# Hyena's inverse transforms in radix-2 steps with tokens in the rows, its bias as a product with ones, and its projection in three passes of 256 columns

## The chip, the cores and the metric

The kernel runs on one core of a Trainium2 chip. The metric is the device time of one execution in microseconds. All data are float32; matmuls take each operand as a pair of rounded parts (high and low).

## What is computed

Two layers of a hybrid backbone over 256 latent tokens of width 2048. Layer 0 (state space and attention) and both FFNs are not touched. Layer 1 is a bidirectional order-2 Hyena long convolution:

```python
proj = dwconv_centred(u @ w_in + b_in, short_w, short_b)      # 3 x 2048 channels, 3 taps
x1, x2, y = proj[..., :d], proj[..., d:2 * d], proj[..., 2 * d:]
for i, gate in enumerate((x1, x2)):
    h_two = einsum('lf,fkd->lkd', hid, fw_out[:, i]) * window
    k = concat(h_two[:, 0], 0, flip(h_two[1:, 1]));  k = k / sum(|k|)
    y = gate * (irfft(rfft(y, 512) * rfft(k, 512))[:256] + fbias[i] * y)
return y @ w_out + b_out
```

## The kernel before

A product of two split operands is three matmuls (`mm3`, lines 372 to 374): high x high, high x low, low x high, added up in one PSUM tile. Weights come from HBM as 1 MB tiles and are split on the chip: ScalarE copies the rounded high part (line 339), VectorE subtracts it (line 340). `run` walks over a list of such tiles; it loads and splits two tiles ahead, and after each tile it advances a list of background generators by some ticks. A generator issues a piece of other work at each `yield`. The build's scheduler orders the instructions of each engine by priority, so pieces of the two streams interleave on TensorE.

There are three forms of a projection tile. `gemm` makes the three passes over 256 (or 258) columns into one accumulator. `wide` (lines 561, 562, 564) takes the high and the low part of the activations side by side as 512 columns against the high weights, and the low weights against 256 columns: two matmuls for each of the 16 blocks of the contraction, and two halves to be added at the end. `total` does that: ScalarE copies one half with the bias (line 573), VectorE adds the other (line 574). `gemm2` (line 819) is layer 0's own.

Layer 1: `ev_hy` makes 48 projection tiles of 128 channels (3 kinds x 16), each followed by the short filter of three taps (lines 1227 to 1229). The first 5 tiles (`HFOLD`) use the unnormalised input with `gemm` and are folded afterwards; 43 use `wide` and `total`. Tiles come in 8 groups of 256 channels. For each group `hyena_steps` runs in the background, once for each of two orders:
- four transposes bring y (channels in rows) to even and odd tokens in rows (line 1263), which are split;
- forward transforms of the even and of the odd tokens (12 matmuls each way, `ps_u`), sum and difference of the two give the two halves of the spectrum (lines 1277, 1278);
- each half is multiplied by the filter's spectrum, read back from HBM, and split into `ph`, `pl`;
- the inverse transform (`ps_c`), with channels in rows: for each of two halves of the channels, 4 spectrum blocks x 3 passes of 256 columns;
- y times the bias on ScalarE (line 1300), the inverse times 1/norm added to it (line 1301), and the gate's product (line 1302), on VectorE.

In the startup a generator `filters` makes the filters of both orders for 4 x 512 channels, 8 rounds: products of 512 columns (`pss`), the window (line 755), splits, the sum of the absolute values (`am`), the spectra (`psk`, in `spectra`), which go to HBM, and 1/norm (`kinv`). It takes turns with generators for the modulation vectors (`ps_mod`), whose weights stream in, and the input norms. The stage after it starts when the filters' memory is free.

The modulation vectors for the later sub-layers are made on VectorE all along the kernel: one multiplication of 128x2048 (line 445) and 1 MB of weights for each 128 channels, 160 in all. `MODS` says how many are issued per 16 blocks of contraction in each of five stages (layer 0's two projections, FFN 0, hyena, FFN 1).

Of the kernel before, what the change touches and what calls it, by code (L numbers as in the profile page):

```python
# [37 lines left out]
MOD_HOLD = 3  # L38
MODS = (1.8, 0.6, 0.68, 0.08, 0.6)
TICKS = ((1, 1, 1), (1, 2), (4,))  # L40
# [131 lines left out]
def _prepare(inputs):  # L172
# [82 lines left out]
    a["hw_out"] = _tiles(g["hy_w_out"][0])  # L255
    fw = g["hy_fw_out"][0]
    a["fw"] = fw.transpose(1, 2, 0, 3).reshape(2, P, 4, 512).transpose(0, 2, 1, 3)
    hid = np.zeros((P, 3 * P), f32)
# [8 lines left out]
class _Kernel:  # L267
# [428 lines left out]
    def filters(self, pool):  # L696
# [31 lines left out]

        yield
        wt = None  # L730
        last = None
# [38 lines left out]
    def spectra(self, pool, fh, fl, gi, s2, am):  # L770

        nc = self.nc
        g, i = gi // 2, gi % 2
        for w in range(2):
            two = []
            for tt in (1, 0):
                ps = self.ps.tile([P, 512], F32, tag=("acc", "ms")[tt], name=self.nm("psk"), bufs=3)
                r = slice(w * P, (w + 1) * P)
                self.mm3(ps, (fh[:, tt, r], fl[:, tt, r]), (s2[w][0][:, tt], s2[w][1][:, tt]), True, True)
                two.append(ps)  # L780
            odd = pool.tile([P, 512], F32, tag="odd", name=self.nm("kodd"), bufs=1)
# [425 lines left out]
    def ev_hy(self, blocks, g, kind, i):  # L1207
# [17 lines left out]
        else:  # L1225
            t = self.total(self.wide(blocks, self.cols_of(self.need_n(self.hn))), self.col("hy_b_in", ci))
        nc.scalar.activation(o, t, AF.Identity, bias=self.col("short_b", ci), scale=self.col("short_w", 48 + ci))
# [22 lines left out]

    def hyena_steps(self, g):
        nc, hp = self.nc, self.hyp
        y = self.hyt[g, 0]
        for o in range(2):
            kf = hp.tile([P, 4, S], F32, tag="kf", name=self.nm("kf"), bufs=1)
            src = self.kscr[2 * (g // 2) + o].rearrange("p (a b) -> p a b", b=512)
            nc.sync.dma_start(kf, src[:, :, (g % 2) * S:(g % 2) * S + S])
            yth = hp.tile([P, 2, S], F32R, tag="yth", name=self.nm("yth"), bufs=1)
            ytl = hp.tile([P, 2, S], F32R, tag="ytl", name=self.nm("ytl"), bufs=1)
            pst = self.ps.tile([P, 2, S], F32, tag="ms", name=self.nm("ps_yT"))  # L1260
            for tt in range(2):
                for c in range(2):
                    nc.tensor.transpose(pst[:, tt, c * P:(c + 1) * P], y[:, c, tt::2], self.mat("ident"))
            self.split(yth, ytl, pst)
            yield from self.wait(1 + HWAITS[0])
# [12 lines left out]
            nc.vector.tensor_tensor(odd, psu[0], odd, ALU.subtract)  # L1278
            for f2, u in enumerate((ev, odd)):
                t = hp.tile([P, 2, S], F32, tag="t1", name=self.nm("t1"), bufs=2)  # L1280
# [3 lines left out]
                nc.vector.tensor_tensor(u[:, 1], u[:, 1], t[:, 0], ALU.add)  # L1284
                self.split(*[v.rearrange("p (r f) t -> p r f t", f=2)[:, :, f2] for v in (ph, pl)], u)
                yield
            yield from self.wait(HWAITS[1])
            while (g, 1 + o, 1) not in self.hy_done:
                yield
            if g == 0 and o == 1:  # L1290
                self.mh, self.ml, self.mhl = self.pair("hmix")
            for c in range(2):
                ch = 2 * g + c
                psc = self.ps.tile([P, 512], F32, tag="ms", name=self.nm("ps_c"))
                cs = slice(c * P, (c + 1) * P)
                for f4 in (0, 2, 1, 3):
                    self.mm3(psc[:, :S], (ph[:, f4, cs], pl[:, f4, cs]), (self.dih[:, f4], self.dil[:, f4]), f4 == 0, f4 == 3)
                yc = y[:, c, :]
                t = self.small.tile([P, S], F32, tag="ft", name=self.nm("yt"), bufs=3)
                nc.scalar.activation(t, yc, AF.Copy, scale=self.col("fbias", o * 16 + ch))  # L1300
                nc.vector.scalar_tensor_tensor(t, psc[:, :S], self.kinv[:, o * 16 + ch:o * 16 + ch + 1], t, ALU.mult, ALU.add)
                nc.vector.tensor_tensor(yc, t, self.hyt[g, 1 + o][:, c, :], ALU.mult)
                if o == 1:
                    self.split(self.mh[:, ch, :S], self.ml[:, ch, :S], yc)
            yield from self.wait(1 + HWAITS[2])
# [238 lines left out]
    def layer1(self):  # L1544
        nc, a, hp = self.nc, self.a, self.hyp
        self.hn = {}
        self.hyt = {}
# [65 lines left out]
```

## Time and profile before

| | |
|---|---|
| median of 3 runs | 2646.43 us (2644.79 to 2648.49) |
| profiled execution, time | 2648.55 us |
| its span | 2646.7 us |
| mean granted TensorE clock | 0.99 |
| startup | 0 to about 190 us |
| layer 0 and FFN 0 | about 190 to 1445 us |
| hyena with its projections | about 1445 to 1806 us |
| output projection and FFN 1 | about 1806 to 2647 us |

The span goes from the first to the last instruction. PE is TensorE's matmul stream, PEld its weight loads, DVE is VectorE, ACT ScalarE, POOL GpSimd and SP SyncE, which issues most DMAs.

### The profile page before, as it was taken

How to read it: one execution, taken by the hardware profiler on the slowest of the kernel's cores; microseconds unless marked ns; L12 is line 12 of the kernel's file. 1: busy time of each engine (PE TensorE's matmuls, PEld its weight loads, DVE VectorE, ACT ScalarE, POOL GpSimd, SP SyncE). 2: the span in 40 equal slices, each digit the busy share in tenths (PEclk: the TensorE clock that was granted, in tenths of full speed). 3: DMA queues.
4: the chain of work that ended last, by engine and by line, in shares of the span. 5: the costliest groups of instructions: out<-in, count | busy, mean ns of one | idle time of the engine just before them, and what ended most of it. 6: DMA issues, size and time to landing. Idle time of an engine off the chain costs nothing.

```text
span 2646.7 us, 39320 instructions
## 1 busy us (share of the span) xinstructions
PE 2572.2 (97%) x15128; PEld 2200.9 (83%) x15128; DVE 2088.8 (79%) x3178; ACT 1428.2 (54%) x2298; POOL 7.4 (0%) x22
## 2 busy tenths in 40 slices
PE   5979999999999999999999999999999999999997
PEld 2548779887988888888888888888998888888886
DVE  7867878777898888888889999898887656656656
ACT  4544656646654544544556755556654544544455
POOL 0000000000000000000000000000000000000000
PEclk9979999999999999999999999999999999999999
DMA  9956557556588887988887555456587654545543
GB/s 354 342 211 221 189 186 278 208 203 234 215 323 310 335 310 284 343 308 298 330 302 271 198 179 180 170 184 235 207 313 261 217 178 169 215 171 195 192 162 125
DMA packets 105610, 635.58 MB, mean 240 GB/s; under 512 B 11344, under 2 KB 19920, under 8 KB 44624
## 3 DMA queue, kind: packets, MB, share of 16 engines
q1 hardware_dynamic: 101904, 620.49, 64.3%
q10 hardware_dynamic: 2304, 8.39, 0.8%
q0 software_dynamic: 1216, 4.20, 0.5%
q8 instruction: 119, 1.95, 0.3%
q14 instruction: 67, 0.55, 0.1%
HBM read 622.55 MB, written 10.49 MB: 239 GB/s over the span
## 4 chain that ended last, share of the span: by engine, by line
PE 92%; DVE 4%; ACT 1%; issue 1%; DMA 1%; SPq 0%; DVEq 0%; ACTq 0%
PE acc L561 41%; PE acc L562 23%; PE acc L819 7%; PE acc L564 3%; PE acc L372 3%; PE acc L373 3%; PE acc L374 3%; PE ps_mod L1383 1%; DVE wlo L340 1%; PE ps_c L372 1%; PE ps_c L374 1%; PE ps_c L373 1%; DVE mraw L445 1%; PE ps_y L1070 0%; PE ps_o L1201 0%
## 5 line engine op out<-in xcount | busy, mean ns | idle before, releaser
L561 PE MATMUL acc<-act,whi 128*128 128x512 f32 x3525 | 1255.6, 396 | 3.9 <-ACT whi L339 3.9
L340 DVE TENSOR_TENSOR wlo<-raw,whi 128x1024 fp32r<-128x1024 f32 (+1 forms) x842 | 938.7, 1119 | 239.1 <-ACT whi L339 232.8
L339 ACT ACTIVATE whi<-raw 128x1024 fp32r<-128x1024 f32 (+1 forms) x842 | 814.6, 972 | 469.7 <-PE acc L561 244.5
L562 PE MATMUL acc<-act,wlo 128*128 128x256 f32 x3760 | 1020.7, 281 | 1.4 <-DVE wlo L340 1.4
L561 PEld LDWEIGHTS acc<-act,whi 128*128 128x128 f32 x3525 | 666.2, 189 | 150.4 <-ACT whi L339 4.9
L562 PEld LDWEIGHTS acc<-act,wlo 128*128 128x128 f32 x3760 | 709.3, 189 | 23.1 <-DVE wlo L340 2.9
L561 PE MATMUL acc<-hh,whi 128*128 128x512 f32 x1280 | 456.4, 395 | 0.0
L445 DVE SCALAR_TENSOR_TENSOR mraw<-mraw,cb 128x2048 f32<-128x2048 f32 x160 | 365.8, 2287 | 30.7 <-DMA mraw<-in_mod 30.4
L562 PE MATMUL acc<-hh,wlo 128*128 128x256 f32 x1408 | 376.2, 282 | 0.0
L561 PEld LDWEIGHTS acc<-hh,whi 128*128 128x128 f32 x1280 | 240.9, 188 | 51.0
L562 PEld LDWEIGHTS acc<-hh,wlo 128*128 128x128 f32 x1408 | 264.7, 188 | 11.5
L571 ACT ACTIVATE sum<-acc 128x256 f32<-128x256 f32 x160 | 61.5, 385 | 271.8 <-PE acc L564 271.8
L372 PE MATMUL acc<-act,whi 128*128 128x258 f32 (+1 forms) x560 | 160.4, 287 | 1.0 <-ACT act L500 1.0
L574 DVE TENSOR_TENSOR sum<-sum,acc 128x256 f32<-128x256 f32 x203 | 85.1, 419 | 96.1 <-ACT sum L571 95.8
L374 PE MATMUL acc<-act,wlo 128*128 128x258 f32 (+1 forms) x560 | 158.4, 284 | 0.9 <-DVE wlo L340 0.9
L373 PE MATMUL acc<-act,whi 128*128 128x258 f32 (+1 forms) x560 | 158.8, 284 | 0.0
L819 PE MATMUL acc<-act,whi 128*128 128x512 f32 x480 | 156.8, 404 | 0.0
L583 ACT ACTIVATE res<-acc,mcol 128x256 f32<-128x256 f32 x144 | 68.2, 474 | 135.5 <-PE acc L564 135.3
L586 DVE SCALAR_TENSOR_TENSOR res<-acc,mcol,res 128x256 f32<-128x256 f32 x160 | 77.1, 483 | 69.2 <-ACT res L583 59.7
L372 PEld LDWEIGHTS acc<-act,whi 128*128 128x128 f32 x560 | 106.6, 191 | 4.0 <-issue 2.5
L374 PEld LDWEIGHTS acc<-act,wlo 128*128 128x128 f32 x560 | 106.4, 190 | 2.0 <-DVE wlo L340 1.1
L373 PEld LDWEIGHTS acc<-act,whi 128*128 128x128 f32 x560 | 106.6, 190 | 1.4 <-issue 0.8
(333 smaller groups left out, 2754.3 us busy)
## 6 DMA issues: line engine op xcount, KB each, us to landing
raw<-in_w SPq DMA_DIRECT2D x176, 1024.0 KB, 4.9
mraw<-in_mod SPq DMA_DIRECT2D x160, 1024.0 KB, 5.1
raw<-in_w SPq DMA_DIRECT2D x128, 704.0 KB, 4.2
raw<-in_hw_in SPq DMA_DIRECT2D x48, 1024.0 KB, 4.8
raw<-in_w_in SPq DMA_DIRECT2D x29, 1024.0 KB, 5.0
mraw<-in_modn SPq DMA_DIRECT2D x19, 1024.0 KB, 9.0
raw<-in_w_o SPq DMA_DIRECT2D x16, 1024.0 KB, 4.8
raw<-in_hw_out SPq DMA_DIRECT2D x16, 1024.0 KB, 4.8
```

The lines of the kernel that those rows point to most:

```text
L339: nc.scalar.activation(hi, src, AF.Copy)
L340: nc.vector.tensor_tensor(lo, src, hi.bitcast(F32), ALU.subtract)
L372: t.matmul(out, lh, rh, start=first, stop=False)
L373: t.matmul(out, lh, rl, start=False, stop=False)
L374: t.matmul(out, ll, rh, start=False, stop=last)
L445: self.nc.vector.scalar_tensor_tensor(raw, raw, 1.0, self.cb, ALU.mult, ALU.mult, accum_out=self.mcol[:, j:j + 1])
L561: t.matmul(*high, start=kt == 0, stop=False, skip_group_check=True)
L562: t.matmul(ps[:, :S], wl, x[:, 0], start=False, stop=False, skip_group_check=True)
L564: t.matmul(*high, start=False, stop=True, skip_group_check=True)
L574: nc.vector.tensor_tensor(v, v, halves[0], ALU.add)
L586: nc.vector.scalar_tensor_tensor(v, halves[0], gate, v, ALU.mult, ALU.add)
L819: t.matmul(ps.rearrange("p (a b) -> p a b", a=2), w, self.act[:, j, :, kt, :S], start=kt == 0 and k == 0, stop=kt == n - 1 and k == 2)
```

## The change

- The inverse transform is done with frequencies against tokens: the two halves of the spectrum are added and subtracted first (VectorE), so that even tokens need only the sum and odd tokens only the difference. The tables, read at every second token, are the stationary operand, the spectra the moving one; tokens come out in the rows.
- Order 0: the gate is transposed to the same layout, multiplied there, and the product is the input of order 1 as it stands. Order 1: the result is transposed back, multiplied by its gate and split.
- The bias term becomes part of the filter's spectrum: bias x sum of absolute values, as a product of a matrix of ones with a row on each partition, is added to the even part of each spectrum. 1/norm is multiplied into the short filter's taps and bias of the two gates.
- `ev_hy` uses `gemm` over 256 columns in place of `wide` and `total`.
- `MODS`: 0.68 to 0.72 in FFN 0, 0.08 to 0 in hyena.

```diff
-MODS = (1.8, 0.6, 0.68, 0.08, 0.6)
+MODS = (1.8, 0.6, 0.72, 0.0, 0.6)
...
+    fb = g["hy_fbias"][0].reshape(2, 4, 512).transpose(1, 0, 2).reshape(8, 1, 512)
+    a["fbrow"] = np.broadcast_to(fb, (8, P, 512))
...
+        self.ones_r = pool.tile([P, P], F32R, name="ones_r")
+        nc.scalar.activation(self.ones_r, self.mat("ones"), AF.Copy)
...
+        fb = pool.tile([P, 512], F32, tag="fwr", name=self.nm("fb"), bufs=2)
+        nc.gpsimd.dma_start(fb, self.a["fbrow"][gi])
+        nc.vector.tensor_tensor(fb, fb, am, ALU.mult)
+        fx = [pool.tile([P, 512], F32R, tag=t, name=self.nm("fx"), bufs=2) for t in ("fwh", "fwl")]
+        self.split(*fx, fb)
...
-                self.mm3(ps, (fh[:, tt, r], fl[:, tt, r]), (s2[w][0][:, tt], s2[w][1][:, tt]), True, True)
+                self.mm3(ps, (fh[:, tt, r], fl[:, tt, r]), (s2[w][0][:, tt], s2[w][1][:, tt]), True, w == 1 or tt == 1)
+                if w == 0 and tt == 0:
+                    for k in range(2):
+                        nc.tensor.matmul(ps, self.ones_r, fx[k], start=False, stop=k == 1)
...
-            t = self.total(self.wide(blocks, self.cols_of(self.need_n(self.hn))), self.col("hy_b_in", ci))
+            ps = self.gemm(blocks, *self.need_n(self.hn)[:2], S)
+            t = self.small.tile([P, S], F32, tag="ft", name=self.nm("sum"), bufs=3)
+            nc.scalar.activation(t, ps[:, :S], AF.Identity, bias=self.col("hy_b_in", ci))
...
+        def by_tokens(v):
             pst = self.ps.tile([P, 2, S], F32, tag="ms", name=self.nm("ps_yT"))
             for tt in range(2):
                 for c in range(2):
-                    nc.tensor.transpose(pst[:, tt, c * P:(c + 1) * P], y[:, c, tt::2], self.mat("ident"))
-            self.split(yth, ytl, pst)
+                    nc.tensor.transpose(pst[:, tt, c * P:(c + 1) * P], v[:, c, tt::2], self.mat("ident"))
+            return pst
+
+        src = by_tokens(self.hyt[g, 0])
+        for o in range(2):
...
+            self.split(yth, ytl, src)
...
-                self.split(*[v.rearrange("p (r f) t -> p r f t", f=2)[:, :, f2] for v in (ph, pl)], u)
                 yield
+            t = hp.tile([P, 2, S], F32, tag="t1", name=self.nm("dif"), bufs=2)
+            nc.vector.tensor_tensor(t, ev, odd, ALU.subtract)
+            nc.vector.tensor_tensor(ev, ev, odd, ALU.add)
+            self.split(*parts[0], ev)
+            self.split(*parts[1], t)
...
+            if o == 0:
+                gate = hp.tile([P, 2, S], F32, tag="t1", name=self.nm("gate"), bufs=2)
+                nc.scalar.activation(gate, by_tokens(self.hyt[g, 1]), AF.Copy)
+            psc = self.ps.tile([P, 2, S], F32, tag="ms", name=self.nm("ps_c"))
+            for tt in range(2):
+                for k, r in enumerate((0, 2)):
+                    w = [d[:, r, tt::2] for d in (self.dih, self.dil)]
+                    self.mm3(psc[:, tt], w, (ph[:, r + tt], pl[:, r + tt]), k == 0, k == 1)
+            if o == 0:
+                nc.vector.tensor_tensor(gate, psc, gate, ALU.mult)
+                src = gate
+                continue
+            yt = hp.tile([P, 2, S], F32, tag="t1", name=self.nm("yt"), bufs=2)
+            nc.scalar.activation(yt, psc, AF.Copy)
+            yield
...
-                for f4 in (0, 2, 1, 3):
-                    self.mm3(psc[:, :S], (ph[:, f4, cs], pl[:, f4, cs]), (self.dih[:, f4], self.dil[:, f4]), f4 == 0, f4 == 3)
-                yc = y[:, c, :]
-                t = self.small.tile([P, S], F32, tag="ft", name=self.nm("yt"), bufs=3)
-                nc.scalar.activation(t, yc, AF.Copy, scale=self.col("fbias", o * 16 + ch))
-                nc.vector.scalar_tensor_tensor(t, psc[:, :S], self.kinv[:, o * 16 + ch:o * 16 + ch + 1], t, ALU.mult, ALU.add)
-                nc.vector.tensor_tensor(yc, t, self.hyt[g, 1 + o][:, c, :], ALU.mult)
-                if o == 1:
-                    self.split(self.mh[:, ch, :S], self.ml[:, ch, :S], yc)
+                for tt in range(2):
+                    nc.tensor.transpose(pst[:, c, tt::2], yt[:, tt, c * P:(c + 1) * P], self.mat("ident"))
+            yc = self.hyt[g, 0]
+            nc.vector.tensor_tensor(yc, pst, self.hyt[g, 2], ALU.mult)
+            for c in range(2):
+                self.split(self.mh[:, 2 * g + c, :S], self.ml[:, 2 * g + c, :S], yc[:, c])
...
+        for v in [self.col("short_w", 48 * k, 32) for k in range(3)] + [self.col("short_b", 0, 32)]:
+            nc.vector.tensor_tensor(v, v, self.kinv, ALU.mult)
```

## Rows read from the trace of the kernel before

**Rows 1.** The page, parts 1 and 4.
```profile
PE 2572.2 (97%) x15128; PEld 2200.9 (83%) x15128; DVE 2088.8 (79%) x3178; ACT 1428.2 (54%) x2298; POOL 7.4 (0%) x22
...
PE 92%; DVE 4%; ACT 1%; issue 1%; DMA 1%; SPq 0%; DVEq 0%; ACTq 0%
```

**Rows 2.** By stage: us, busy time of each engine, granted clock, DMA share, GB/s.
```profile
20.00:60.00 40.00, 31.72 (x118) 13.91 (x119) 31.36 (x72) 23.33 (x51) 1.07 (x2) 0.91 0.91 357
60.00:110.00 50.00, 46.59 (x248) 25.91 (x247) 42.73 (x85) 25.51 (x44) 2.14 (x4) 1.00 0.97 369
110.00:160.00 50.00, 33.93 (x164) 17.98 (x162) 36.15 (x70) 25.02 (x40) 0.19 (x2) 0.84 0.67 247
...
190.00:1410.00 1220.00, 1214.25 (x7156) 1048.02 (x7155) 1011.31 (x1444) 654.64 (x1053) 0.52 (x4) 1.00 0.74 270
1410.00:1440.00 30.00, 29.12 (x170) 25.41 (x169) 27.63 (x46) 19.25 (x36) 0.00 (x0) 1.00 0.70 245
1440.00:1480.00 40.00, 38.00 (x283) 35.64 (x282) 38.57 (x73) 29.85 (x58) 0.00 (x0) 1.00 0.59 224
...
1500.00:1790.00 290.00, 289.93 (x1809) 257.38 (x1808) 267.61 (x460) 163.71 (x254) 0.00 (x0) 1.00 0.50 178
```

**Rows 3.** Timeline of PE, one tile of hyena's projection, first and last step.
```profile
1624.19 0.39 PE L561 MATMUL acc<-act,whi 128*128 128x512 f32 x1
...
1629.13 0.39 PE L561 MATMUL acc<-act,whi 128*128 128x512 f32 x1
```

**Rows 4.** Timeline of PE, layer 0's z projection, eighteen steps apart.
```profile
424.91 0.28 PE L372 MATMUL acc<-act,whi 128*128 128x256 f32 x1
...
431.35 0.28 PE L372 MATMUL acc<-act,whi 128*128 128x256 f32 x1
```

**Rows 5.** Timeline of PE, inverse transform, first and last of 24.
```profile
1613.53 0.28 PE L372 MATMUL ps_c<-dih,ph 128*128 128x256 f32 x1
...
1616.28 0.28 PE L374 MATMUL ps_c<-dih,pl 128*128 128x256 f32 x1
```

**Rows 6.** Timeline of PE, four transposes and what follows.
```profile
1630.30 0.65 PE L1263 MATMUL ps_yT<-mats,hyt 128*128 128x128 f32 x4
1630.70 0.36 PE L374 MATMUL ps_c<-dih,pl 128*128 128x256 f32 x1
1630.90 0.28 PE L372 MATMUL ps_c<-dih,ph 128*128 128x256 f32 x1
```

**Rows 7.** Groups by line and shape, 1500 to 1790 us: busy, mean ns, idle before.
```profile
L373 PEld LDWEIGHTS ps_c<-dil,ph 128*128 128x128 f32 x117 | 22.2, 190 | 0.4
...
L574 DVE TENSOR_TENSOR sum<-sum,acc 128x256 f32<-128x256 f32 x39 | 16.2, 416 | 0.0
...
L1301 DVE SCALAR_TENSOR_TENSOR yt<-ps_c,kinv,yt 128x256 f32<-128x256 f32 x30 | 14.2, 481 | 0.7 <-PE ps_c L374 0.4
...
L1277 DVE TENSOR_TENSOR even<-ps_u,odd 128x512 f32<-128x512 f32 x14 | 9.6, 687 | 5.6 <-ACT odd L1275 5.5
...
L445 DVE SCALAR_TENSOR_TENSOR mraw<-mraw,cb 128x2048 f32<-128x2048 f32 x4 | 9.1, 2287 | 0.0
...
L1275 ACT ACTIVATE odd<-ps_u 128x512 f32<-128x512 f32 x14 | 8.3, 592 | 8.3 <-PE ps_u L374 8.3
```

**Rows 8.** Groups by line and shape, 0 to 190 us.
```profile
L339 ACT ACTIVATE fwh<-fwr 128x512 fp32r<-128x512 f32 x8 | 5.0, 626 | 4.4 <-PE pss L374 4.0 <-DMA fwr<-in_fw 0.4
```

**Rows 9.** The chain in the startup: start us, us, what.
```profile
28.36 0.43 PE pss L372
...
67.24 0.23 PE psk L374
...
157.63 2.50 ACT act L1456 x6
```

**Rows 10.** VectorE's timeline in the startup.
```profile
67.49 1.89 DVE L340 TENSOR_TENSOR sl<-sv,sh 128x512 fp32r<-128x512 f32 x3
```

**Rows 11.** The chain at the start of hyena.
```profile
1461.92 2.21 DVE mraw L445 x2
```

**Rows 12.** Groups by line and shape, 1400 to 1850 us.
```profile
L455 DVE TENSOR_TENSOR mcol<-mcol,cols 128x16 f32<-128x16 f32 x1 | 0.2, 171 | 0.0
```

More of the change, by code (lines that the diff above doesn't have):

```diff
@@ L1252, in hyena_steps @@
         nc, hp = self.nc, self.hyp
[L1253 to L1259, printed above, removed]
+        def by_tokens(v):
             pst = self.ps.tile([P, 2, S], F32, tag="ms", name=self.nm("ps_yT"))
@@ L1262, in hyena_steps @@
                 for c in range(2):
-                    nc.tensor.transpose(pst[:, tt, c * P:(c + 1) * P], y[:, c, tt::2], self.mat("ident"))
-            self.split(yth, ytl, pst)
+                    nc.tensor.transpose(pst[:, tt, c * P:(c + 1) * P], v[:, c, tt::2], self.mat("ident"))
+            return pst
+        src = by_tokens(self.hyt[g, 0])
+        for o in range(2):
+            kf = hp.tile([P, 4, S], F32, tag="kf", name=self.nm("kf"), bufs=1)
+            scr = self.kscr[2 * (g // 2) + o].rearrange("p (a b) -> p a b", b=512)
+            nc.sync.dma_start(kf, scr[:, :, (g % 2) * S:(g % 2) * S + S])
+            yth = hp.tile([P, 2, S], F32R, tag="yth", name=self.nm("yth"), bufs=1)
+            ytl = hp.tile([P, 2, S], F32R, tag="ytl", name=self.nm("ytl"), bufs=1)
+            self.split(yth, ytl, src)
             yield from self.wait(1 + HWAITS[0])
@@ L1278, in hyena_steps @@
             nc.vector.tensor_tensor(odd, psu[0], odd, ALU.subtract)
-            for f2, u in enumerate((ev, odd)):
+            both = (ev, odd)
+            parts = [[v.rearrange("p (r f) t -> p r f t", f=2)[:, :, f2] for v in (ph, pl)] for f2 in range(2)]
+            for f2, u in enumerate(both):
                 t = hp.tile([P, 2, S], F32, tag="t1", name=self.nm("t1"), bufs=2)
@@ L1289, in hyena_steps @@
                 yield
-            if g == 0 and o == 1:
+            if o == 0:
[13 more added lines that the diff above has]
+            yield
+            if g == 0:
                 self.mh, self.ml, self.mhl = self.pair("hmix")
+            pst = self.ps.tile([P, 2, S], F32, tag="ms", name=self.nm("ps_yC"))
             for c in range(2):
-                ch = 2 * g + c
-                psc = self.ps.tile([P, 512], F32, tag="ms", name=self.nm("ps_c"))
-                cs = slice(c * P, (c + 1) * P)
-                for f4 in (0, 2, 1, 3):
-                    self.mm3(psc[:, :S], (ph[:, f4, cs], pl[:, f4, cs]), (self.dih[:, f4], self.dil[:, f4]), f4 == 0, f4 == 3)
-                yc = y[:, c, :]
-                t = self.small.tile([P, S], F32, tag="ft", name=self.nm("yt"), bufs=3)
-                nc.scalar.activation(t, yc, AF.Copy, scale=self.col("fbias", o * 16 + ch))
-                nc.vector.scalar_tensor_tensor(t, psc[:, :S], self.kinv[:, o * 16 + ch:o * 16 + ch + 1], t, ALU.mult, ALU.add)
-                nc.vector.tensor_tensor(yc, t, self.hyt[g, 1 + o][:, c, :], ALU.mult)
-                if o == 1:
-                    self.split(self.mh[:, ch, :S], self.ml[:, ch, :S], yc)
+                for tt in range(2):
[4 more added lines that the diff above has]
+                self.split(self.mh[:, 2 * g + c, :S], self.ml[:, 2 * g + c, :S], yc[:, c])
             yield from self.wait(1 + HWAITS[2])
```

## The prediction, as written before the result was known

> **What bounds the kernel now.** I read the page first: TensorE is busy 97% of the span, and 92% of the chain that ended last is TensorE's [rows 1]. So the price of most edits is TensorE time, but only in stages where it really is the bound. The table by stage says where [rows 2]. From 190 to 1410 us, and in the hyena stage from 1500 to 1790, TensorE is busy for 99.5% and 100% while VectorE stands at 83% and 92%. In the startup (20 to 160 us) no engine is full: VectorE has 78%, 85% and 72% of its three stretches, TensorE 79%, 93% and 68%, and the DMA share is 0.91, 0.97 and 0.67. From 1410 to 1480, where the first FFN ends and hyena begins, VectorE has 92% and 96%, TensorE misses 1 and 2 us, and the chain of waits there runs over VectorE, as at 1461.92 [rows 11]. The change touches three of these stages, each with its own limit.
>
> A matmul's shown duration includes its pipeline (a 256-column one shows 0.28 us), so I price TensorE by the distance from one start to the next.
>
> **Hyena's projection.** One contraction step was a 512-column and a 256-column matmul; it becomes three of 256, so 768 columns either way and one instruction more. Fourteen old steps go from 1624.19 to 1629.13: 0.353 us a step [rows 3]. The same three-pass form stands in layer 0's z projection: eighteen steps from 424.91 to 431.35, 0.3578 us [rows 4]. The first 5 of 48 tiles already used the folded three-pass form, so 43 tiles x 16 steps x 4.9 ns = **+3.4 us**, bounds +2.5 and +4.3 for the rounding of the four starts. A rule of the Trainium skill speaks against this part: TensorE: Matmul & The Clock Gate, section Back-to-back issue gap, gives about 81 ns a matmul at 128 columns and 131 at 512 as the sustained rate with a weight load ahead of each; an estimate from it at 256 is 98, so 229 ns would become 293 and the part would cost +44 us. The rows show 119 ns for 256 columns (a third of 0.3578) and 234 for 512 (0.353 less that) instead of 98 and 131, so the trace doesn't agree and I go by the rows.
>
> With the three passes in one accumulator, one ScalarE pass evicts it with the bias and the VectorE addition (0.416 us [rows 7]) is gone from 43 tiles. TensorE doesn't wait for it in this stage, so it is worth nothing directly; it pays for VectorE work below.
>
> **The inverse transforms.** Per group of 256 channels and per order, the old code did 2 halves x 4 blocks x 3 passes = 24 matmuls of 256 columns; the radix-2 form does 2 x 2 x 3 = 12. Twenty-four in a row start from 1613.53 to 1616.28, so 0.1196 us each [rows 5]. 8 groups x 2 orders x 12 x 0.1196 = **-23.0 us**. The stationary operand is now the table read at every second column; the old forward transposes read their operand at every second token and start 0.12 us apart [rows 6], so I add nothing for the stride and keep doubling as the other bound (a rival below).
>
> With tokens in the rows, the gate has to be transposed too (order 0: 4 more), and the result transposed back (order 1: 4, in place of the 4 that turned y before order 1). Net 4 more per group, 32 in all. Four in a row push the next work from 1630.30 to 1630.70 and the matmul behind them takes 0.20 instead of 0.12: 0.48/4 = 0.12 us [rows 6]. The new ones come in fours: 32 x 0.12 = **+3.8 us**; bounds 3.2 (0.40/4 each) and 7.7, twice that, should each stand alone and break the stream. The Trainium skill (TensorE: Matmul & The Clock Gate, Part 4: PE-mode transpose) has about 275 ns for one in a kernel; by that the term would be 8.8, and the 0.12 of this trace doesn't agree.
>
> VectorE per group: minus 6 x 0.416 of the projection; minus 4 x (0.481 + 0.42) of the old tail of the inverses, plus 2 x 0.687 for the new products; plus 4 x 0.687 for the sum and difference of the two half spectra [rows 7]: -2.5 - 3.6 + 1.4 + 2.7 = -2.0 us. The weight multiplications for modulation (2.29 us each, four in this stretch [rows 7]) go too. A group takes TensorE 96 x 0.353 + 72 x 0.1196 + 8 x 0.12 = 43.5 us now and 96 x 0.3578 + 48 x 0.1196 + 12 x 0.12 = 41.5 after, and VectorE at 92% of 43.5 less 2.0 and 1.1 is 36.9, or 89%. ScalarE loses four passes of 256 columns and gains two of 512, at 56% [rows 2]. So the stage should stay bound by TensorE, and the 15.8 us (-23.0 + 3.8 + 3.4) should be seen in the span. If TensorE begins to wait here, the cover for the new VectorE work is gone; that is a rival.
>
> **The modulation rates.** 0.68 to 0.72 in the first FFN: its 132 units of work issue 5.3 more multiplications; 0.08 to 0 in hyena: 3.8 fewer. In the FFN they lie under TensorE (VectorE 83%), their DMAs of 1 MB under a share of 0.74 [rows 2]. In its last 16 tasks VectorE is the bound, and 16 x 11/16 x 0.04 x 2.29 = **+1.0 us**. On SP's queue each is one more load ahead of weights, with the same cover. At hyena's start one multiplication stands on the chain at 1461.92 for 2.21 us with only VectorE work around it [rows 11]; it goes. The scaling of the short filter by 1/norm puts four small VectorE instructions (128x32) in front of the stage; nothing of that shape is in the trace, so between 0.17 each (a 128x16 one [rows 12]) and 0.42 (a 128x256 one [rows 7]), less the 0.09 by which neighbours overlap [rows 10]; nearer the small, 4 x 0.1 = 0.4, upper bound 1.3. Together **-1.8 us**.
>
> **The bias in the filter spectrum.** Eight times: a 256 KB load on POOL's queue, a VectorE product and a VectorE subtraction of 128x512 (0.69 shown; three in a row take 1.89, so 0.60 apart [rows 10]), a ScalarE copy (0.63 [rows 8]), two 512-column matmuls (0.43 each on the chain at 28 us, 0.23 at 67 us [rows 9]); once, a copy of the ones. Before, the bias was a ScalarE pass in hyena, under cover. Here the startup waits alternately for all of these, and everything after waits for the end of the filters. One bound: all hidden in the idle time of three engines, 0. The other: all serial, 8 x (1.20 + 0.63 + 2 x 0.43) = 21.5 us. Between them: DMA alone, 2.1 MB at the 369 GB/s of the fullest stretch, 5.7 us; VectorE alone, 9.6 us, of which a part falls into the 15 to 28% that it has free. The load shares POOL's queue and the two buffers of the filter weights, so the next group's weights can be asked for only when the last bias is consumed; from the chain's 28.36 to 157.63, where the next stage begins [rows 9], a group lasts 16 us, so I expect no wait. I take **+7**.
>
> **Sum.** +3.4 - 23.0 + 3.8 + 1.0 - 1.8 + 7.0 = -9.6 us. The profiled execution had a span of 2646.7 and a time of 2648.55, the runs a median of 2646.43 (2644.79 to 2648.49); I take it off the median, 0.3 under the span: 2636.8, so **2637**. About 0.2% (5.3 us) is what a measurement of this kernel can tell from no change.
>
> **Rivals.**
> - *The startup hides the filter's new work*, since its engines are 68 to 93% busy. Then -16.6: 2630. Against it: VectorE at 85% and a DMA share of 0.97 in the fullest stretch [rows 2].
> - *TensorE starts to wait in hyena.* The second order follows the first without a pause: product, ScalarE copy, VectorE remainder, then the forward matmuls. If VectorE 0.69 and ScalarE 0.59 [rows 7] stood open once in each group, 8 x 1.28 = 10 us come back: 2647, no change. For it: VectorE at 89%; against it: TensorE idle for under 0.1 us of 290 now [rows 2].
> - *The startup pays in series*: with 0.23 a matmul, 8 x (1.20 + 0.63 + 2 x 0.23) = 18.3 instead of 7 gives 2648, no change; with 0.43 a matmul, 21.5 gives 2651.5. For it: the chain there hops between all three engines; against it: each has free time.
> - *The other side: the strided stationary operand loads at half rate.* Each of the 192 remaining inverse matmuls would take 0.24 instead of 0.12: +23, so 2660, slower. It decides from 78 ns each, (9.6 + 5.3)/192. Against it: the strided transposes at 0.12.
> - *More passes cost more than columns*: a weight load shows 0.19 us [rows 7], 71 ns more than the 119 between matmuls of 256. If that stuck out once in each step that gets a third pass, 688 x 71 ns = +49 in place of +3.4: 2682. Against it: the z projection runs three loads a step at 0.3578. By the issue gap of the Trainium skill cited above (TensorE: Matmul & The Clock Gate, Back-to-back issue gap), an estimate for this case is 2677.5; the trace doesn't agree with it.
>
> **Chances.** Forecast 0.50 (2632 to 2643 by its own bounds), startup hidden 0.15, waits in hyena 0.13, startup in series 0.12, strided loads 0.07, pass cost 0.03. Faster takes the hidden startup and 0.46 of the forecast: 0.61. Same takes the rest of the forecast, the waits, and 0.09 of the series case: 0.26. Slower: 0.13. The range leaves out strided loads, pass cost, and the far ends of the others: 2629 to 2649.
>
> **What would show it.** TensorE: 192 ps_c matmuls instead of 384, 0.12 apart; 96 transposes; a projection step of 0.358. The hyena stretch from its first tile to the last about 17 us shorter, VectorE near 89% and TensorE still without idle time. The filters ending some 7 us later than 157 us. If the hyena stretch shrinks by less than 10, a wait is there, and its releaser will be ScalarE's yth or VectorE's product; if the startup grows by over 14, the sum is wrong there.

## The result, and where the time went

The changed kernel takes 2664.35 us in the median of 6 runs (2661.34 to 2669.24) against 2646.72 us of the kernel before (2643.16 to 2648.49): 1.0071 times as long, 95% interval 1.006 to 1.0082. It was forecast 9.6 us faster and is 17.6 us slower. The profiled execution took 2661.34 us, with a span of 2659.6.

I set the two traces side by side by the same events: the first `ps_dup` matmul (layer 0 has its norms), the start of the reciprocal of each later norm (FFN 0, hyena, FFN 1, the last one), and the start of the last residual of hyena's output projection on ScalarE.

| stretch, us | before | after | after less before | forecast |
|---|---|---|---|---|
| startup, 0 to first `ps_dup` | 202.0 | 218.5 | +16.5 | +7.0 |
| layer 0 to FFN 0's norm | 500.1 | 504.3 | +4.2 | 0 |
| FFN 0, norm to norm | 747.2 | 749.3 | +2.1 | +1.0 |
| hyena, norm to last residual | 440.0 | 429.4 | -10.6 | |
| its rest, to FFN 1's norm | 6.9 | 8.7 | +1.8 | |
| hyena in all | 446.9 | 438.0 | -8.9 | -17.6 |
| FFN 1, norm to norm | 739.2 | 738.1 | -1.1 | 0 |

The sum, +12.9, is the difference of the spans (2659.6 - 2646.7); the medians lie 4.7 further apart, since the profiled execution of the changed kernel is its shortest run and that of the kernel before is longer than all six of its own. The page, parts 1 and 4 (answers to [rows 1]):

```profile
PE 2573.7 (97%) x15672; PEld 2226.4 (84%) x15672; DVE 2088.9 (79%) x3139; ACT 1429.8 (54%) x2291; POOL 11.7 (0%) x30
...
PE 88%; DVE 7%; DMA 2%; issue 2%; ACT 1%; SPq 0%; DVEq 0%; ACTq 0%; POOLq 0%
```

TensorE has the same busy time on a longer span, and 4 points of its share of the chain have gone to VectorE, to DMA and to issue. By stage (answers to [rows 2]; columns as there):

```profile
20.00:60.00 40.00, 31.73 (x124) 13.74 (x124) 32.76 (x74) 23.26 (x51) 0.54 (x1) 0.96 0.94 366
60.00:110.00 50.00, 41.48 (x209) 23.40 (x207) 37.65 (x74) 21.61 (x37) 3.75 (x7) 0.90 0.90 327
110.00:160.00 50.00, 41.27 (x184) 24.34 (x179) 44.16 (x85) 28.79 (x45) 3.22 (x6) 0.90 0.64 232
...
1500.00:1790.00 290.00, 288.79 (x2348) 282.07 (x2347) 260.86 (x418) 170.92 (x255) 0.00 (x0) 1.00 0.51 176
```

In the startup no engine became full: from 60 to 110 us TensorE and VectorE are both less busy than before, 41.5 instead of 46.6 and 37.7 instead of 42.7, and the granted clock is 0.90 instead of 1.00. So new waits stand there. The lower clock explains little of the longer startup: from 0 to the first `ps_dup` its mean is 0.91 before and 0.90 after, and two kernels with one startup (the first of experiment 4, the second of experiment 6) take 206.1 and 206.0 us at 0.93 and 0.91. In hyena TensorE, which had missed 0.07 us of 290, misses 1.2; VectorE is at 90%.

**The startup's waits.** The waits from 55 to 175 us (engine, line, waited for: us in all, times, longest):

```profile
ACT fx L341 <- DVE fb L781: 11.6, 5, 5.4
...
POOL fb L780 <- DVE fx L342: 9.8, 1, 9.8
DVE fb L781 <- DMA fb<-in_fbrow: 9.7, 3, 5.0
```

VectorE stands still for 9.7 us for the bias row, and POOL once waits 9.8 us for the last reader of its ring buffer (`fx`) before it can ask for the next row. VectorE's timeline shows the longest of these waits (in brackets: idle before, releaser):

```profile
93.49 0.17 DVE L805 RECIPROCAL kinv<-psl 128x4 f32<-128x4 f32 x1
93.58 0.66 DVE L342 TENSOR_TENSOR fwl<-fwr,fwh 128x512 fp32r<-128x512 f32 x1
99.20 0.69 DVE L781 TENSOR_TENSOR fb<-fb,am 128x512 f32<-128x512 f32 x1 [4.96 <-DMA fb<-in_fbrow]
```

The chain of waits has the transfer behind it (start us, us, what):

```profile
86.98 3.31 issue
...
90.31 8.80 DMA fb<-in_fbrow
...
99.40 0.41 issue
99.81 0.69 DVE sv L759
```

POOL asks for the row only when the two-buffer ring that it shares with the filter weights turns over; it lands 8.80 us after its issue, and VectorE, which works in order, holds back the window product behind it (99.81 us in the timeline). The filters' end, which was at 157.63 us [rows 9], is at 175.19:

```profile
165.13 8.20 DMA kscr<-ko
173.42 1.30 DVE ko L798 x2
175.19 9.68 ACT act L1493 x24
```

**The rest of hyena.** After the last residual the changed kernel has one multiplication for the modulation left, on VectorE ahead of FFN 1's norm at 1910.1 us; the kernel before has none there. With the rates alone (experiment 5) it stands there too, so these 1.8 us are the rates'.

```profile
1906.71 2.29 DVE L447 SCALAR_TENSOR_TENSOR mraw<-mraw,cb 128x2048 f32<-128x2048 f32 x1 [1.21 <-DMA mraw<-in_mod]
```

**Hyena's matmuls.** A projection step, eight of them between these starts (answers to [rows 3]): 2.87/8 = 0.359 us. The new inverse, eleven matmuls in a row from the first row to the last (answers to [rows 5]): 1.32/11 = 0.12 us.

```profile
1625.06 0.28 PE L374 MATMUL acc<-act,whi 128*128 128x256 f32 x1
...
1627.93 0.28 PE L374 MATMUL acc<-act,whi 128*128 128x256 f32 x1
...
1633.95 0.28 PE L375 MATMUL ps_c<-pl,dih 128*128 128x256 f32 x1
...
1635.15 0.28 PE L376 MATMUL ps_c<-ph,dil 128*128 128x256 f32 x1
1635.27 0.28 PE L375 MATMUL acc<-act,whi 128*128 128x256 f32 x1
```

The weight load of a table read at every second column shows 196 ns where the plain one showed 190 [rows 7] (minimum, median, maximum, first and last start):

```profile
L375 PEld LDWEIGHTS ps_c<-pl,dih x64: 192/196/206, 1522.6 to 1815.3; 128*128 128x128 f32 x64
```

The distances from each TensorE start to the next, added up from hyena's norm to the last residual by the tile that the earlier one writes (a wait counts with the matmul ahead of it), give the whole stretch:

| us | before | after | difference | forecast |
|---|---|---|---|---|
| `ps_c` | 48.1 | 24.3 | -23.8 | -23.0 |
| transposes | 6.7 | 10.9 | +4.2 | +3.8 |
| projections | 360.9 | 369.0 | +8.1 | +3.4 |
| `ps_u` | 24.2 | 25.3 | +1.1 | 0 |
| sum | 439.9 | 429.4 | -10.5 | -15.8 |

### The profile page after: what moved, and what is told of

It is laid out like the page before. It is cut to its first block, busy times and chain, and to the rows that moved or that the text cites. A ratio compares the mean times of both kernels' runs of the same rounds, so it can differ in the third digit from the quotient of the medians.

```text
span 2659.6 us, 40325 instructions
## 1 busy us (share of the span) xinstructions
PE 2573.7 (97%) x15672; PEld 2226.4 (84%) x15672; DVE 2088.9 (79%) x3139; ACT 1429.8 (54%) x2291; POOL 11.7 (0%) x30
## 4 chain that ended last, share of the span: by engine, by line
PE 88%; DVE 7%; DMA 2%; issue 2%; ACT 1%; SPq 0%; DVEq 0%; ACTq 0%; POOLq 0%
PE acc L563 34%; PE acc L564 19%; PE acc L832 7%; PE acc L376 5%; PE acc L374 5%; PE acc L375 5%; PE acc L566 3%; DVE wlo L342 1%; PE ps_mod L1420 1%; DVE mraw L447 1%; DMA mraw<-in_mod 1%; PE ps_y L1083 0%; PE ps_u L374 0%; DMA x<-in_xT 0%; DVE acc L492 0%
## 5 line engine op out<-in xcount | busy, mean ns | idle before, releaser
L563 PE MATMUL acc<-act,whi 128*128 128x512 f32 x2880 | 1024.2, 396 | 5.7 <-ACT whi L341 4.2
L564 PE MATMUL acc<-act,wlo 128*128 128x256 f32 x3072 | 833.2, 281 | 2.8 <-DVE wlo L342 2.7
L563 PEld LDWEIGHTS acc<-act,whi 128*128 128x128 f32 x2880 | 544.0, 189 | 127.0 <-ACT whi L341 4.7
L374 PE MATMUL acc<-act,whi 128*128 128x256 f32 (+1 forms) x1248 | 353.8, 284 | 0.1
L376 PE MATMUL acc<-act,wlo 128*128 128x256 f32 (+1 forms) x1248 | 352.0, 283 | 1.1 <-DVE wlo L342 0.9
L375 PE MATMUL acc<-act,whi 128*128 128x256 f32 (+1 forms) x1248 | 351.7, 282 | 1.2 <-DVE act L503 1.0
L374 PEld LDWEIGHTS acc<-act,whi 128*128 128x128 f32 x1248 | 236.3, 190 | 3.2 <-issue 2.5
L375 PEld LDWEIGHTS acc<-act,whi 128*128 128x128 f32 x1248 | 235.9, 189 | 3.2 <-DVE act L503 1.5
L832 PE MATMUL acc<-act,whi 128*128 128x512 f32 x480 | 157.8, 406 | 0.0
L576 DVE TENSOR_TENSOR sum<-sum,acc 128x256 f32<-128x256 f32 x160 | 67.1, 419 | 96.4 <-ACT sum L573 96.3
```

Source lines behind the costliest of these rows:

```text
L374: t.matmul(out, lh, rh, start=first, stop=False)
L375: t.matmul(out, lh, rl, start=False, stop=False)
L376: t.matmul(out, ll, rh, start=False, stop=last)
L563: t.matmul(*high, start=kt == 0, stop=False, skip_group_check=True)
L564: t.matmul(ps[:, :S], wl, x[:, 0], start=False, stop=False, skip_group_check=True)
L832: t.matmul(ps.rearrange("p (a b) -> p a b", a=2), w, self.act[:, j, :, kt, :S], start=kt == 0 and k == 0, stop=kt == n - 1 and k == 2)
```

## The experiments

Each kernel was timed in turns with the kernel before, whose median was 2645.85 to 2646.54 us; the number of the new kernel's runs stands in brackets. A ratio is to the kernel before, with its 95% interval. A trace is one execution: in the five of kernels with the old startup it takes 199.5 to 202.0 us, in the three with the changed kernel's own 218.4 to 220.7, so a difference of 2 us in it isn't told by one trace.

**1. What the filter's bias costs.** Two kernels: rows asked for three rounds ahead, and no bias in the spectrum at all.

```diff
+            nc.gpsimd.dma_start(self.cb[:, gi % 4 * 512:(gi % 4 + 1) * 512], a["fbrow"][gi])
...
-        fb = pool.tile([P, 512], F32, tag="fwr", name=self.nm("fb"), bufs=2)
-        nc.gpsimd.dma_start(fb, self.a["fbrow"][gi])
+        fb = self.cb[:, gi % 4 * 512:(gi % 4 + 1) * 512]
```

> The bias rows get buffers of their own (the modulation vector's tile, empty until the startup ends) and are asked for three rounds ahead. Theory: of the 16.5 us by which the startup grew, 9.7 are VectorE waiting for these loads, so the filters end 7 to 10 us earlier, at 165 to 168 us instead of 175, and the time falls from 2664 to about 2655. Rival (the new work itself, or its 2.1 MB on full DMA queues, makes the startup longer): no load is waited for, the filters still end at 172 us or later, and the time stays within 3 us of 2664.

Measured: 2660.09 us (5 runs), 1.0051 [1.0038, 1.0063]. VectorE no longer waits for a row, the startup is 215.4 us instead of 218.5. The 9.7 us of waits were worth 4.3 in the median (the two intervals just touch, at 1.0060 to 1.0063) and 3.1 in the trace. The filters still end at 172.78 us, as the rival had it, though the time falls by a little more than its 3 us. So the theory that the waits carry the slowdown falls: the work itself costs most.

```diff
-        nc.vector.tensor_tensor(fb, fb, am, ALU.mult)
-        fx = [pool.tile([P, 512], F32R, tag=t, name=self.nm("fx"), bufs=2) for t in ("fwh", "fwl")]
-        self.split(*fx, fb)
...
-                if w == 0 and tt == 0:
-                    for k in range(2):
-                        nc.tensor.matmul(ps, self.ones_r, fx[k], start=False, stop=k == 1)
```

> The bias term is left out of the filter's spectrum (no load, product, split or matmul for it); hyena stays as changed. Theory: the filters end at 157.6 us again and the time is 2664 less 16.5, about 2648: the other parts together are worth nothing against before, since layer 0 lost 4.5 us and the end of the first FFN 2, and hyena gained 10.7 only. Rival (the 4.5 us in layer 0 came from the later start): 2642 to 2644, faster than before.

Measured, without the load, the product, its two parts, the two matmuls and the matrix of ones: 2642.77 us (11 runs), 0.9988 [0.9979, 0.9996]. So the bias costs 2664.35 - 2642.77 = 21.6 us, and all the rest of the change together gains 3. The startup is back at 200.7. The time is the rival's, its reason only in part: of the 4.2 us of layer 0, 2.3 come back.

**2. Hyena's projection and the rates, undone in the changed kernel.**

```diff
-            ps = self.gemm(blocks, *self.need_n(self.hn)[:2], S)
-            t = self.small.tile([P, S], F32, tag="ft", name=self.nm("sum"), bufs=3)
-            nc.scalar.activation(t, ps[:, :S], AF.Identity, bias=self.col("hy_b_in", ci))
+            t = self.total(self.wide(blocks, self.cols_of(self.need_n(self.hn))), self.col("hy_b_in", ci))
```

> Only hyena's projection goes back to the 512 + 256 form with the sum on VectorE. Theory: a step costs 4.9 ns less, 3.4 us in all, and TensorE has cover, so 2661. Rival (VectorE, with 18 us more to do, becomes the bound of hyena): 2666 to 2675, with TensorE waiting for VectorE in hyena.

Measured: 2667.84 us (4 runs), 1.0082 [1.0068, 1.0095]. The time doesn't fall by 3.4, it rises by 3.5, as the rival had it, though its interval reaches into that of the changed kernel. The trace shows waits that fit (TensorE's weight loads from 1500 to 1830 us, first of this kernel, then of the changed one, then of the kernel before):

```profile
PEld acc L564 <- DVE wlo L342: 8.3, 11, 1.5
PEld ps_c L374 <- ACT ph L341: 4.1, 8, 2.1
```

```profile
PEld acc L376 <- DVE wlo L342: 2.6, 7, 0.5
PEld acc L564 <- DVE wlo L342: 2.0, 2, 1.4
```

```profile
PEld acc L562 <- DVE wlo L340: 0.8, 4, 0.2
```

Line 564 (562 before) is the low part of the wide form: with 43 additions of 0.416 us [rows 7] back on VectorE, the weights' remainders come late eleven times, 8.3 us; the changed kernel shows 2.6 and 2.0. The kernel before, with the same additions but the old inverses, shows 0.8, so the additions alone don't do it.

```diff
-MODS = (1.8, 0.6, 0.72, 0.0, 0.6)
+MODS = (1.8, 0.6, 0.68, 0.08, 0.6)
```

> Only the modulation rates go back to 0.68 and 0.08. Theory: the end of the first FFN gets 2 us shorter and hyena's front 2 us longer: 2664, no change. Rival (the higher rate starves the FFN of weights): 2660 or less.

Measured: 2668.43 us (5 runs), 1.0085 [1.0071, 1.0098]: 4.1 above the changed kernel, again with overlapping intervals, and neither what the theory nor what the rival had. In its trace FFN 0 takes 2.6 us less (746.7) and hyena up to the last residual 7.9 more (437.3), with seven multiplications of 2.29 us there where the changed kernel has none: half of their VectorE time. Norm to norm hyena takes 6.3 more, since the multiplication left for its end is gone.

**3. What in the bias costs the other 17 us.** Four variants of the kernel with early rows, to tell apart VectorE's time, the chain of dependent steps, and the bytes.

```diff
-        nc.vector.tensor_tensor(fb, fb, am, ALU.mult)
+        nc.gpsimd.tensor_tensor(fb, fb, am, ALU.mult)
...
-        self.split(*fx, fb)
+        nc.scalar.activation(fx[0], fb, AF.Copy)
+        nc.gpsimd.tensor_tensor(fx[1], fb, fx[0], ALU.subtract)
```

> The changed kernel with the bias rows asked for early, and the product and the subtraction of the bias made on GpSimd in place of VectorE. Early rows alone left 2660, 13 us more than before. Theory 1, VectorE's time carries them: the 9.6 us of VectorE work leave it, so the startup gets at least 5 us shorter and the time is 2651 to 2655. Theory 2, the chain of dependent steps in front of the spectrum's matmul carries them (product, copy, subtraction, two matmuls, one after the other): the same chain is there, each GpSimd step as long or longer, so 2659 to 2665. Theory 3, the 2.1 MB of rows: as early rows, 2660.

Measured: 2662.98 us (5 runs), 1.0058 [1.0045, 1.0071]. No gain, as theory 2 had it; but the run doesn't test theory 1, since it has a second reason. VectorE's and GpSimd's timelines:

```profile
113.36 1.38 DVE L342 TENSOR_TENSOR sl<-sv,sh 128x512 fp32r<-128x512 f32 x1
...
118.99 0.68 DVE L342 TENSOR_TENSOR sl<-sv,sh 128x512 fp32r<-128x512 f32 x1
```

```profile
112.93 1.26 POOL L781 TENSOR_TENSOR cb<-cb,am 128x512 f32<-128x512 f32 x1 [4.91 <-DVE am L768]
```

GpSimd takes 1.26 us for a product that VectorE does in 0.69, and a VectorE subtraction beside it takes 1.38 instead of 0.68. The Trainium skill (SBUF — State Buffer, section SBUF: two separate sides) says that VectorE with two SBUF inputs and a GpSimd operation that reads SBUF share a pair of ports, which whichever starts first holds for its whole instruction; this trace agrees, with 0.70 us longer for VectorE where GpSimd's product had another 0.83 us to run (112.93 + 1.26 - 113.36). In all, the six VectorE instructions with two SBUF inputs that start during GpSimd's work are 5.4 us longer; those that read PSUM beside it keep their 0.68 us.

```diff
-        for w in range(2):
+        for w in (1, 0):
...
-            if w == 0:
+            if w == 1:
                 yield
```

> The changed kernel with early bias rows, and the two halves of a spectrum in the other order: the half without the bias first, so that a yield and six matmuls lie between the bias product and the matmul that needs it. Theory 1 (VectorE's time): the same work, so 2658 to 2661. Theory 2 (the chain of steps): the chain is covered by the other half, so 2650 to 2655. Theory 3 (the rows' bytes): 2660.

Measured: 2653.13 us (8 runs), 1.0027 [1.0017, 1.0037]: 7 us less than with early rows alone, with the same instructions, bytes and engines: the price of the order. It is shown by the medians; in the traces the startup gets 2.3 us shorter (213.1), no more than such traces differ by. In the kernel with early rows the chain of waits goes through its links one after the other (product, copy, the spectrum's matmuls with the ones):

```profile
117.97 0.61 DVE cb L781
118.60 0.64 ACT fx L341
119.28 0.79 PE psk L792
```

and its waits show who stood behind them, TensorE and then VectorE's `ko`:

```profile
PEld psk L792 <- ACT fx L341: 2.4, 1, 2.4
...
DVE ko L798 <- PE psk L792: 1.8, 3, 1.2
```

With the other order the second of these waits is gone, and TensorE waits for the two parts of the product (`fx`) for 1.5 us instead of 2.8, most of it for VectorE's part:

```profile
PEld psk L792 <- DVE fx L342: 1.0, 1, 1.0
```

```diff
-        fx = [pool.tile([P, 512], F32R, tag=t, name=self.nm("fx"), bufs=2) for t in ("fwh", "fwl")]
-        self.split(*fx, fb)
...
-                    for k in range(2):
-                        nc.tensor.matmul(ps, self.ones_r, fx[k], start=False, stop=k == 1)
+                    nc.tensor.matmul(ps, self.mat("ones"), fb, start=False, stop=True)
```

> The changed kernel with early bias rows and the product not split: one matmul of the float32 ones with the float32 product, in place of the ScalarE copy, the VectorE subtraction and two matmuls of rounded parts. VectorE loses 8 x 0.6 = 4.8 us, ScalarE 5 us, the chain of steps two links of 0.6; the float32 matmul takes TensorE longer than the two it replaces (no row of before has that shape; by as much as two rounded ones if it is four passes: 0.5 us, 4 us in all). Theory 1: 2656 to 2658. Theory 2: 2652 to 2656. Theory 3: 2660. If TensorE's time counts most there, 2661 to 2664.

Measured: 2654.4 us (8 runs), 1.0027 [1.0017, 1.0038]: 5.7 us less than with early rows alone, with a chain two links shorter. The two links are also work that is gone, 0.6 us each eight times, and this run doesn't tell the one from the other.

```diff
-            nc.gpsimd.dma_start(self.cb[:, gi % 4 * 512:(gi % 4 + 1) * 512], a["fbrow"][gi])
...
-        nc.vector.tensor_tensor(fb, fb, am, ALU.mult)
+        nc.vector.tensor_tensor(fb, am, am, ALU.mult)
```

> The changed kernel without the load of the bias rows: the product takes the sums of absolute values twice, so all work stays and no bytes come (the bias is replaced by these sums). Theory 3 (the 2.1 MB slow the modulation weights, whose loads take a share of 0.95 to 1.0 of the DMA engines from 20 to 120 us): 2653 to 2656, the 5.7 us that the bytes take at 369 GB/s. Theories 1 and 2: 2658 to 2661, as with early rows.

Measured: 2656.35 us (5 runs), 1.0039 [1.0026, 1.0052]: 3.7 less, but the interval overlaps that of early rows alone, so the bytes' share isn't settled by the medians. In the traces the startup is as long without the load, 215.3 us, as with it, 215.4.

**4. The bias at its cheapest.** The diffs of early rows, the other order and the unsplit product together; then with the last diff above as well, without the load of the rows.

> The changed kernel with three edits of the bias together: rows asked for early, the half of the spectrum without the bias first, and the product not split (one float32 matmul). Theory 2, the chain of steps in front of the spectrum's matmul carries most of it: the first two edits alone gave 2653.1, early rows with the unsplit product 2654.4; what is left of the chain is one VectorE product that the other half covers, so 2648 to 2652, and the rest over the version without any bias (2642.8) is the 2.1 MB and 8 products. If the two edits cover the same wait, 2653 again.

Measured: 2651.08 us (11 runs), 1.0019 [1.001, 1.0028]. 13.3 us of the 21.6 are back; the startup takes 206.1 us, 4.1 more than before.

> The three edits of the bias without the load of its rows (the product takes the sums of absolute values twice, in place of the bias). Without any bias 2642.8 was measured, with the three edits 2651.1: 8.3 us are left. Theory 3 (the 2.1 MB): the load carries 4 us of them, as it did with early rows alone (2660.1 to 2656.4), so 2646 to 2648. Rival, the loads are covered once the chain is short: 2650 to 2652, and the rest is the product's 4.8 us of VectorE and the float32 matmul.

Measured: 2649.97 us (11 runs), 1.0014 [1.0005, 1.0023]. No effect of the rows' bytes can be told once the chain is short. What is left over the version without bias, 7 to 8 us, is the product, the float32 matmul and their dependences; these I didn't take apart.

**5. The two other parts, in the kernel before.** From the change's own diff: the lines of `ev_hy`, the line of `MODS`, and both.

> The kernel before with the three-pass projection alone. The prediction's sum: +3.4, so 2650. Theory V, VectorE holds TensorE up in hyena although it is only 92% busy (it works in order, and the weights' remainders stand behind the background's work): 43 additions of 0.416 us go, 17.9 us of VectorE, and the change was 3.5 us slower without this part, so 2640 to 2644.

Measured: 2649.41 us (11 runs), 1.0013 [1.0004, 1.0022]: +3.5, where the prediction's term was +3.4. Theory V falls for the kernel before: a relief of 17.9 us of VectorE is worth nothing there. In its trace hyena, norm to norm, takes 3.8 us more (450.7).

> The kernel before with the new modulation rates alone. The prediction's sum: +1.0 and -2.2, so 2645. Theory V: four multiplications of 2.29 us leave hyena's VectorE and the change was 4 us slower with the old rates, so 2641 to 2644.

Measured: 2647.06 us (11 runs), 1.0007 [0.9998, 1.0016]: no difference that can be told. In the trace FFN 0 gets 4.2 us longer (751.4) and hyena 4.2 shorter (442.7): the rates move the price and save none.

> The kernel before with the three-pass projection and the new rates, old inverses and no new filter work. The prediction's sum: 2648 to 2649. Theory V: 2637 to 2642 if the two gains add up, 2641 to 2643 if the second finds VectorE already free. This would be the first version faster than both kernels.

Measured: 2652.87 us (9 runs), 1.0028 [1.0018, 1.0037]: the gains that theory V added up don't exist here. The time lies above that of either part, though its interval reaches into that of the first.

**6. Hyena's rate alone**, with FFN 0's at 0.68, in the kernel before and in the first one of experiment 4.

```diff
+MODS = (1.8, 0.6, 0.68, 0.0, 0.6)
```

> The kernel before with hyena's rate alone: no multiplications in hyena, FFN 0 as it was. With both rates changed FFN 0 took 751.4 us from norm to norm instead of 747.2, and hyena 433.9 instead of 440.0. Theory V (VectorE holds TensorE up in hyena): hyena again near 434, FFN 0 near 747, so 2638 to 2642, the first version faster than both kernels. The prediction's sum: -2.2, so 2644. Rival: the multiplications that hyena doesn't make are made up at its front or at the next norm, then 2645 to 2647.

> The changed kernel with the three edits of the bias (early rows, the half without it first, product not split) and FFN 0's old rate, hyena's new one. FFN 0 took 2.6 us less with the old rate in the changed kernel: 2651.1 - 2.6 = 2648.5, so 2647 to 2650. Rival: FFN 0's end is bound by VectorE either way, 2651.

Measured: 2661.89 us (5 runs), 1.0067 [1.0053, 1.008], and 2668.79 us (4 runs), 1.0084 [1.0071, 1.0098]. Neither theory holds; the rival of the first was right in kind and its price far too small. VectorE's timeline of the first kernel, its table by stage, SyncE's and TensorE's timelines, and the chain of waits:

```profile
1795.94 2.29 DVE L445 SCALAR_TENSOR_TENSOR mraw<-mraw,cb 128x2048 f32<-128x2048 f32 x1
...
1802.89 2.28 DVE L445 SCALAR_TENSOR_TENSOR mraw<-mraw,cb 128x2048 f32<-128x2048 f32 x1
```

```profile
1500.00:1770.00 270.00, 270.00 (x1689) 240.43 (x1688) 244.32 (x424) 154.41 (x239) 0.00 (x0) 1.00 0.47 166
1770.00:1830.00 60.00, 42.37 (x245) 36.24 (x244) 50.38 (x79) 25.98 (x41) 0.00 (x0) 0.86 0.67 248
```

```profile
1776.06 22.54 SPq L438 DMA_DIRECT2D mraw<-in_mod  x5
...
1819.40 1.22 PE L561 MATMUL acc<-act,whi 128*128 128x512 f32 x2 [15.64 <-ACT whi L339]
```

```profile
1811.24 2.29 DVE mraw L445 x2
1813.56 4.71 DMA raw<-in_hw_out
1818.29 1.06 ACT whi L339
```

The multiplications that hyena doesn't make are due at its end: six start from 1782.7 to 1811.2 us, and TensorE idles 17.6 of 60 us. Of these, 15.64 are one wait for a weight tile of the output projection. The modulation's 1 MB tiles take their buffers from the weights' ring and their turn in SyncE's queue (L438 among L344): no weight tile is asked for between 1770.03 and 1802.66 us, and the one that TensorE stands for only at 1813.56, when the sixth multiplication has ended. FFN 0's 0.72 is what makes hyena's 0 possible; they are one edit. No version that I ran with its bias in place beats the kernel before.

## Why the prediction was wrong, point by point

- **The bias in the spectrum (+7): the step that failed.** It cost 21.6 us by experiment 1. In the traces the startup is 16.5 us longer than before, over the 14 from which the prediction called the sum wrong there. Two sentences were wrong. "So I expect no wait" took the length of a round (16 us) for the slack of a load; the load waits for its ring buffer and then takes up to 8.80 us, and VectorE stood 9.7 us. And "a part falls into the 15 to 28% that it has free" priced the work by the idle share of an engine. Experiment 3 shows that the order counts: the same work cost 7 us less when something else stood between the product and its use. The rival of the startup in series, at 0.12, was the nearest case, and that its bound of 21.5 meets the 21.6 is in part luck: 4.3 of these are the wait for the rows, which it didn't have, and 9.0 more went with the order and the unsplit product while nearly all of the work stayed (2660.09 to 2651.08). The other 8.3 are not taken apart.
- **The inverses (-23.0) and the transposes (+3.8): right**, -23.8 and +4.2. The rivals of the strided load and of the pass cost fell: 0.12 us a matmul, 0.359 a step. The Trainium skill's rate for back-to-back matmuls, which the prediction weighed (TensorE: Matmul & The Clock Gate, Back-to-back issue gap), stays in disagreement with these rows, at 0.12 us for 256 columns. The Trainium skill's 275 ns for a transpose (TensorE: Matmul & The Clock Gate, Part 4: PE-mode transpose) are near the duration that one shows here (`ps_yC`, median 0.273 us); the prediction set them against a distance, which is 10.9/96 = 0.11 us in the stream.
- **The three-pass projection (+3.4): right where it was priced**, in the kernel before (+3.5, experiment 5), and by the medians of the other sign in the changed one (experiment 2, not clear of the noise; hyena, norm to norm, 440.9 us without it, 438.0 with it). There a group gives TensorE less work, and VectorE is late for the weights. "So it is worth nothing directly" holds for the one and not for the other. That a sum of parts, each priced in the old context, misses such a crossing is the second weakness of the sum.
- **Hyena's stretch (-17.6): half of it came**, -8.9. The test that the prediction set (less than 10: a wait is there) is met by 8.9 for the stage, of which the multiplication left at its end took 1.8. The releaser that counts most is not one that it named: it is the low part of a split on VectorE, `wlo` of the weights or `act` of the mixed result, behind the group's other work. The largest of it is at the end, where the last group has no projection beside it (by stage, first before, then after, and TensorE's timeline):

```profile
1790.00:1820.00 30.00, 30.00 (x180) 26.23 (x179) 28.45 (x49) 16.86 (x27) 0.00 (x0) 1.00 0.67 249
```

```profile
1790.00:1820.00 30.00, 27.36 (x191) 25.00 (x191) 23.79 (x40) 14.62 (x23) 0.00 (x0) 1.00 0.48 171
```

```profile
1810.26 0.39 PE L564 MATMUL acc<-act,wlo 128*128 128x256 f32 x1 [1.07 <-DVE wlo L342]
...
1818.89 0.50 PE L563 MATMUL acc<-act,whi 128*128 128x512 f32 x1 [1.57 <-DVE act L342]
```

  TensorE idles 2.64 of 30 us there. The -1.8 at hyena's front can't be told from the drift of the norms between the stages.
- **The rates (+1.0 in FFN 0): too small.** In the traces of all twelve kernels with 0.72 FFN 0 takes 748.3 to 752.2 us, mean 750.2; in the five with 0.68 744.6 to 747.2, mean 745.6: 4.6 us. What makes it 4.6 these runs don't show. In return hyena got 2.2 by the prediction, and from norm to norm got 6.3 in the changed kernel (experiment 2) and 4.2 in the one before (experiment 5). The count was too small as well: FFN 0 makes six multiplications more (94 for 88), and hyena six fewer between its norm and the next (1 for 7), not 5.3 and 3.8.
- **Layer 0 (0): +4.2 unforeseen**, and shown only in part. TensorE's busy time there is 2.3 us longer (496.6 for 494.3), which fits a lower clock, and it idles 1.9 more (7.7 for 5.8). Layer 0 takes 500.0 to 500.1 us in the three kernels with neither the rows' load nor FFN 0's 0.72, 501.7 to 502.6 in the five with 0.72 alone, 503.6 to 505.5 in the nine with the load. Two stretches of 20 and 10 us have a lower granted clock than before (us, busy time of each engine, clock; first before, then after):

```profile
220.00:240.00 20.00, 20.00 (x110) 16.85 (x109) 15.10 (x31) 7.58 (x10) 0.00 (x0) 1.00 0.67 243
600.00:610.00 10.00, 7.95 (x38) 6.57 (x37) 5.39 (x12) 5.14 (x11) 0.00 (x0) 0.83 0.65 233
```

```profile
236.50:256.50 20.00, 20.00 (x102) 16.67 (x102) 14.57 (x31) 7.55 (x10) 0.00 (x0) 0.91 0.64 218
620.00:630.00 10.00, 7.76 (x32) 6.47 (x33) 4.34 (x12) 4.00 (x8) 0.00 (x0) 0.66 0.53 187
```

  Without the rows' load the first is gone:

```profile
233.30:253.30 20.00, 20.00 (x110) 16.85 (x109) 14.63 (x31) 7.58 (x10) 0.00 (x0) 1.00 0.66 241
```

  All nine kernels with that load show it (59.8 to 59.9 us from the first `ps_dup` to the first `ps_y` matmul), none of the eight without it does (58.3). Why a load that ended 80 us and more earlier does that stays open. The second also stands in the kernel before with the new rates alone (0.72 from 600 to 612 us), so it isn't the bias alone; in it TensorE waits for weights for 3.22 us at 622.24, where before it was 2.05 at 602.22. Its cause stays open too.

## What to carry to other kernels

Where engines take turns, work isn't hidden by their idle shares: lay out the chain of the new steps and ask what stands between each result and its first use; putting independent work there was worth 7 us in the medians for two lines, and getting a load out of a shared two-buffer ring another 4. A part that is priced at nothing because another engine is the bound has to be priced again with all the other parts in place. And a rate that moves work to a later stage needs a look at when that work is due, and at whose loads its own then stand ahead of.

## What the runs showed of the hardware

A VectorE subtraction with both inputs in SBUF took 1.38 us instead of 0.68 beside a GpSimd product, which took 1.26: the work that went to the idle engine slowed the busy one. A stationary operand read at every second column costs 6 ns of shown load time (196 for 190) and nothing in the distance of the matmuls. And the float32 matmul of 512 columns that took the place of two rounded ones is two instructions of 0.43 us in the chain of experiment 4's first kernel, at a granted clock of 1.00 (64 to 72 us), where a rounded one takes 0.23 [rows 9]:

```profile
68.02 0.86 PE psk L789 x2
```

The unsplit form gained all the same, with two links of the chain and their work gone.
